# A hybrid decoder step on one core: norm of the first group on its products, banks and weight buffers shared out anew, two output projections moved forward

## The chip, the cores and the metric

The kernel runs on 1 core of a Trainium2 chip. The time is device microseconds of one execution; the kernel before has a median of 2943.49 us over 3 runs (2937.61 to 2943.66).

## What is computed

One layer of a decoder over 2048 prompt rows and 64 sample rows, in fp32. Sandwich norms stand around two sub-layers: a token mixer (windowed attention beside an RWKV-7 recurrence, both fed by one projection and joined by one output projection) and a gated FFN with a causal width-3 convolution. Cut to the lines that the change touches:

```python
hn = _rms_norm(x, g_pre_mix)
proj = hn @ w_in                       # q, k, v, and the RWKV columns
...                                    # attention, window 128; RWKV-7, state 64 x 64
mix = jnp.concatenate([o_attn, o_rw], axis=-1) @ w_out
x = x + _rms_norm(mix, g_post_mix)
f, new_conv = _conv_ffn(_rms_norm(x, g_pre_ffn), conv_prev, w_ffn_in, conv_w, conv_b, w_ffn_out)
x = x + _rms_norm(f, g_post_ffn)
```

`_rms_norm` divides each row by the root of its mean square and multiplies each column by a gain. The division is one factor per row, so it may as well be applied to the rows of `hn @ w_in`; the gain may not.

## The kernel before

**Tiling.** The 2112 rows are cut into five groups g0 to g4, four of 448 rows and one of 320. For each group there are stages: P (projection, 20 tiles), O (output projection, 8 tiles) and FFN, the latter as a main stage of 60 tiles and a last stage of 6. In the code `P[g]`, `O[g]`, `F[2g]` (main) and `F[2g+1]` (last); here P0 to P4, O0 to O4, F0 to F9. A tile is 24 matmuls: 8 steps of depth 128, each with three products (high and low halves of activations and weights, `split`, L348 to L351: ScalarE rounds, VectorE subtracts). `Dense.run` (L357) goes through the tiles in the order of the list `order` (L1581). It loads raw weights (`raw`, three buffers of tag "w"), splits them one tile ahead (`halves`, two buffers each of "wh" and "wl"), and splits the eight activation slices of the next stage while the last tile of the stage before runs (`piece`). Products are gathered in PSUM banks of tag "z" (two) in `gemm` (L433) and in `down` of the FFN, and the function `end` or `take` reads them out on ScalarE or VectorE.

**Mixer.** Eight units (256 prompt rows each, `Mixer.unit`) and one for the sample rows are written as generators. Their PSUM tiles have tag "a" (three banks) and "o" (two); tag "y" (one) serves the side work of the dense stages. That is 8 banks in all.

**Order of the work.** `Flow` decides while the program is written: after each step of a dense tile, `tick` (L254) may put in one step of side work and one of a mixer unit. A unit is paced over a window of the dense work (`windows`, L1588) and starts when the one before it is through. `force` (L266) runs side and mixer steps unpaced until a condition holds. Two tiles ahead of a stage `run` forces its conditions (L398 to L401): a P stage needs its norm's row factors (`"rb" in st`), an O stage needs the mixer units of its rows (L1579), an FFN stage needs its group's O stage done. The rest of an O or a last FFN stage (row norm, gain, residual, second norm; `rest`, L779 and L884) is side work: eight times about three VectorE instructions, then eight more. The instructions so written are then put in order per engine by a list scheduler with its own model of times, the earlier-written first among those that it takes to be ready; at run time each engine goes through its list strictly in order.

**Start.** `norm` of P0 (L472) loads x row-wise in pieces through three small buffers ("r"), squares and sums, takes the inverse roots, spreads them over partitions with a matmul (`rb_ps`), and only then are the first slices of the transposed x scaled by gain and row factor (`scale`, L503), split and multiplied.

**Names and lines.** L183 is every matmul, L350 and L351 the two halves of a split, L503 `scale`, L627 and L630 `shift` after a projection tile, L789 and L797 the rest of an O stage, L861 the FFN's `take`, L1219 the reading of attention scores out of PSUM, L956 the reading of the recurrence's.

Of the kernel before, what the change touches and what calls it, by code (L numbers as in the profile page):

```python
# [18 lines left out]
D = 1024  # L19
# [61 lines left out]
class Shared:  # L81
# [26 lines left out]
    def derived(self):  # L108
# [35 lines left out]
        self.nconv = cp.tile([128, NF, DB, 2], F32, name="nconv")  # L144
        self.zcar = cp.tile([128, NF, 2], F32, name="zcar")
# [154 lines left out]
class Stage:  # L300


    def __init__(self, n, cond=always, begin=None, cond2=always):
        self.n, self.cond, self.begin, self.cond2 = n, cond, begin, cond2
        self.fetch = self.piece = None
        self.tasks, self.xhi, self.xlo, self.raw = [], [], [], []

# [4 lines left out]
class Dense:  # L312
# [10 lines left out]
    def ps(self, name, tag="y"):  # L323
        return self.pp.tile([128, 512], F32, tag=tag, name=name, bufs={"z": 2, "y": 1}[tag])

# [6 lines left out]
    def W(self, name, shape=(D,)):  # L332
        return self.sp.tile([128] + list(shape), F32, tag="w", name=name, bufs=3)

# [22 lines left out]
    def run(self, stages):  # L357
# [18 lines left out]
        def halves(i):  # L376
            if i < nt and i not in parts:
                raw(i)
                parts[i] = [view(i, self.sp.tile([128, D], F32R, tag=x, name=x, bufs=2)) for x in ("wh", "wl")]
                self.split(*parts[i], raws[i])  # L380

        first = stages[0]
        first.begin()
        yield first.cond2
        for k in range(3):
            first.fetch(k)
        for j in range(3):
            raw(j)
        halves(0)
        for k in range(KT):  # L390
            first.piece(k)
            yield None
        for i, t in enumerate(tasks):
            n1, n2, n6 = [starts.get(i + j) for j in (1, 2, 6)]
            if n6 and n6.begin:
                n6.begin()
            if n2:
                yield n2.cond  # L398
                yield n2.cond2
                if n2.piece:  # L400
                    yield from self.hold()  # L401
                    for k in range(3):
                        n2.fetch(k)
            wh, wl = parts[i]
            for k, _ in enumerate(t.run(wh, wl)):
# [6 lines left out]
                yield None  # L412

    def source(self, s, src, then=None):


        def fetch(k):
            if k < KT:
                s.raw.append(self.r(s.n))
                self.nc.sync.dma_start(out=s.raw[k], in_=src(k))  # L420

        def piece(k):
# [3 lines left out]
            hi, lo = [self.sp.tile([128, GW], F32R, tag=z, name=z, bufs=9)[:, :s.n] for z in ("xhi", "xlo")]  # L426
            self.split(hi, lo, x)
            s.xhi.append(hi), s.xlo.append(lo)
            fetch(k + 3)

        s.fetch, s.piece = fetch, piece

    def gemm(self, s, src, end, m=None):  # L433


        def run(wh, wl):
# [3 lines left out]
            for k in range(KT):  # L440
# [3 lines left out]
                if k == KT - 1:  # L444
                    end(ps)
                yield

        s.tasks.append(Task(src, run, m))


    def project(self, g):
# [5 lines left out]
        if sample:  # L457
            segs.append(Seg(npr, NS, DB, DS, DS, npr // CH, sh.sshift, sh.nshift, sh.SEC))
        ks, st, left = [], {}, [0]

# [11 lines left out]
        def norm():  # L472
# [3 lines left out]
            cuts = [0, GW, 2 * GW, D]  # L476
            yield from self.hold()
            for i in range(nt):
                xts = []
                for x, y in zip(cuts, cuts[1:]):  # L480
                    xts.append(self.r(y - x))
                    nc.sync.dma_start(out=xts[-1][:w], in_=a["x"][t0 + w * i:t0 + w * i + w, x:y])
                yield 3000
                for j, xt in enumerate(xts):
                    nc.scalar.activation(out=xt[:w], in_=xt[:w], func=AF.Square, accum_out=ss[:w, j, i:i + 1])
            self.held = False
            yield 1000
            for j in range(2):
                v.tensor_tensor(out=ss[:w, 0, :nt], in0=ss[:w, 0, :nt], in1=ss[:w, j + 1, :nt], op=ALU.add)
            rsqrt(nc, self.sp, rs[:w, :nt], ss[:w, 0, :nt], 1.0 / D, RMS_EPS, nt, w, "nrp")  # L490
# [8 lines left out]

        S = Stage(n, begin=lambda: self.flow.spawn(norm()), cond2=lambda: "rb" in st)  # L500
# [4 lines left out]
        self.source(S, lambda k: a["xT"][:, k, t0:t0 + n], scale)  # L505

# [11 lines left out]
        def key(p):  # L518
            def end(ps):
                ks.append(self.shift(segs, p, ps, self.A("k", n)))  # L520
                if p == 3:
# [7 lines left out]
        def norms():  # L529
            k2s = []  # L530
            for p in range(4):
                k2s.append(self.B("k2", [n]))
# [69 lines left out]

        tile = lambda i, end: self.gemm(S, a["w_all"][i], end)
        self.gemm(S, a["w_l"][:, :, 0:64], lora, 64)
        for p in range(4):
            tile(p, key(p))
        self.gemm(S, a["w_l"][:, :, 64:160], gate, 96)
        tile(12, rotary(0))
# [199 lines left out]
    def ffn(self, g):  # L808
# [8 lines left out]
        def gate(f):  # L817
            def end(ps):
# [16 lines left out]
                if sample:  # L835
                    nc.gpsimd.tensor_copy(out=sh.nconv[:, f], in_=zs[:, :, DS:DS + 2])
                nc.scalar.activation(out=c, in_=c, func=AF.Silu)  # L837
# [74 lines left out]
    def finish(self):  # L912
        self.nc.sync.dma_start(out=self.a["o_conv"], in_=self.sh.zcar)
        self.nc.sync.dma_start(out=self.a["o_conv_s"], in_=self.sh.nconv)


class Mixer:
# [16 lines left out]
    def ps(self, name, tag="a"):  # L934
        return self.pp.tile([128, 512], F32, tag=tag, name=name, bufs={"a": 3, "o": 2}[tag])

# [624 lines left out]
def program(tc, nc, a, seq):  # L1561
    with tc.tile_pool(name="xd", bufs=1, space=DRAM) as xd, tc.tile_pool(name="dp", bufs=2, space=DRAM) as dp, \
# [6 lines left out]
        dn = Dense(sh, flow, (dnp, pd))  # L1569
        mx = Mixer(sh, dn, (mip, pm, dp))  # L1570
        with tc.high_priority(-100):
            sh.load(nc.sync, "sel", "blockones", "wkmask", "amask", "sink", "g_up", "smask", "samask", "ssink", "sshift", "gT", "cw", "sconv")
            sh.stacks(dn.W)
        gs, nu = groups(seq), seq // T
# [13 lines left out]
        windows = [(f(P[1], 0), f(P[1], 1)), (f(P[2], 0), f(P[2], 0.9)), (f(P[3], 0.3), f(F[0], 0.45)), (f(F[0], 0.45), f(F[0], 0.93)),  # L1588
                   (f(F[2], 0), f(F[2], 0.47)), (f(F[2], 0.47), f(F[2], 0.93)), (f(F[4], 0), f(F[4], 0.93)), (f(F[6], 0), f(F[6], 0.6))]
# [21 lines left out]
```

## Time and profile before

| | |
|---|---|
| median of 3 runs | 2943.49 us (2937.61 to 2943.66) |
| the profiled execution | 2943.48 us, its span 2941.7 us |
| TensorE matmul busy | 2775.8 us, 94% of the span, 16993 matmuls |
| VectorE busy | 1925.4 us, 65% |
| ScalarE busy | 1409.3 us, 48% |
| mean granted TensorE clock | 0.968 |

Busy time of TensorE is a union of pipelined instructions, so 94% is not 94% of its peak; what a stretch loses is better read from the number of matmuls in it. The granted clock is given as a share of 2.4 GHz; the other level is 1.2 GHz (0.5).

### The profile page before, as it was taken

How to read it: one execution, taken by the hardware profiler on the slowest of the kernel's cores; microseconds unless marked ns; L12 is line 12 of the kernel's file. 1: busy time of each engine (PE TensorE's matmuls, PEld its weight loads, DVE VectorE, ACT ScalarE, POOL GpSimd, SP SyncE). 2: the span in 40 equal slices, each digit the busy share in tenths (PEclk: the TensorE clock that was granted, in tenths of full speed). 3: DMA queues.
4: the chain of work that ended last, by engine and by line, in shares of the span. 5: the costliest groups of instructions: out<-in, count | busy, mean ns of one | idle time of the engine just before them, and what ended most of it. 6: DMA issues, size and time to landing. Idle time of an engine off the chain costs nothing.

```text
span 2941.7 us, 46311 instructions
## 1 busy us (share of the span) xinstructions
PE 2775.8 (94%) x16993; PEld 2358.6 (80%) x16993; DVE 1925.4 (65%) x3782; ACT 1409.3 (48%) x2644; POOL 250.9 (9%) x519
## 2 busy tenths in 40 slices
PE   6998998999999998989999997999998999998997
PEld 4877766777887897768879886889876888997997
DVE  5776885795584557966836568355586566458566
ACT  5455545546445344655553445443444443344443
POOL 1001010020000000210100000000000000101111
PEclk9998999999999999999999998999998999999998
DMA  6575645766444335655443445433346434346443
GB/s 197 167 213 155 185 135 163 219 197 184 148 136 131 119 125 178 195 157 166 126 134 116 136 147 164 147 112 117 123 126 212 136 110 125 108 137 215 151 146 116
DMA packets 311555, 446.59 MB, mean 152 GB/s; under 512 B 118664, under 2 KB 240424, under 8 KB 311312
## 3 DMA queue, kind: packets, MB, share of 16 engines
q1 hardware_dynamic: 310896, 443.48, 49.5%
q8 instruction: 134, 2.20, 0.3%
q14 instruction: 93, 0.76, 0.1%
q10 hardware_dynamic: 432, 0.16, 0.0%
HBM read 362.19 MB, written 76.97 MB: 149 GB/s over the span
## 4 chain that ended last, share of the span: by engine, by line
PE 76%; DVE 13%; DMA 4%; ACT 3%; issue 3%; SPq 1%; DVEq 0%; ACTq 0%; POOL 0%; POOLq 0%
PE gm L183 47%; PE pf L183 16%; PE pc L183 2%; DVE wl L351 2%; PE po L183 1%; DVE tmp L994 1%; DVE tt L995 1%; PE pz L183 1%; PE ppt L187 1%; DMA r<-od 1%; ACT wh L350 1%; PE sc_e L183 1%; PE pu L183 1%; PE pS L183 1%; PE ms L183 1%
## 5 line engine op out<-in xcount | busy, mean ns | idle before, releaser
L183 PE MATMUL gm<-xhi,wh 128*128 128x448 f32 (+3 forms) x2880 | 1063.8, 371 | 39.3 <-ACT xhi L350 20.1
L183 PE MATMUL gm<-xhi,wl 128*128 128x448 f32 (+3 forms) x2880 | 1039.6, 362 | 16.0 <-DVE wl L351 15.8
L183 PE MATMUL gm<-xlo,wh 128*128 128x448 f32 (+3 forms) x2880 | 1040.6, 362 | 4.3 <-DVE xlo L351 4.0
L350 ACT CAST wh<-w 128x1024 fp32r<-128x1024 f32 (+1 forms) x470 | 488.9, 1040 | 791.7 <-PE gm L183 386.0
L351 DVE TENSOR_TENSOR wl<-w,wh 128x1024 fp32r<-128x1024 f32 (+1 forms) x470 | 570.3, 1213 | 442.6 <-ACT wh L350 441.7
L183 PEld LDWEIGHTS gm<-xhi,wh 128*128 128x128 f32 (+2 forms) x2880 | 546.4, 190 | 121.8 <-ACT xhi L350 31.4
L183 PEld LDWEIGHTS gm<-xhi,wl 128*128 128x128 f32 (+2 forms) x2880 | 546.1, 190 | 74.7 <-DVE wl L351 23.8
L183 PEld LDWEIGHTS gm<-xlo,wh 128*128 128x128 f32 (+2 forms) x2880 | 546.8, 190 | 60.4 <-DVE xlo L351 13.0
L183 PE MATMUL pf<-hh,wh 128*128 128x448 f32 (+1 forms) x880 | 324.8, 369 | 20.7 <-DVE acc L861 20.1
L183 PE MATMUL pf<-hl,wh 128*128 128x448 f32 (+1 forms) x880 | 315.0, 358 | 0.0
L183 PE MATMUL pf<-hh,wl 128*128 128x448 f32 (+1 forms) x880 | 314.5, 357 | 0.0
L834 POOL COPY zcar<-zz 128x2 f32<-128x2 f32 x110 | 82.3, 749 | 1533.9 <-ACT zz L823 1533.9
L183 PEld LDWEIGHTS pf<-hh,wh 128*128 128x128 f32 x880 | 166.6, 189 | 47.1 <-DVE acc L861 24.7
L861 DVE TENSOR_TENSOR acc<-acc,pf 128x448 f32<-128x448 f32 (+1 forms) x200 | 117.8, 590 | 100.1 <-PE pf L183 98.9
L183 PEld LDWEIGHTS pf<-hh,wl 128*128 128x128 f32 x880 | 167.0, 190 | 13.2 <-issue 1.8
L183 PEld LDWEIGHTS pf<-hl,wh 128*128 128x128 f32 x880 | 167.0, 190 | 12.2 <-issue 2.2
L844 DVE TENSOR_TENSOR c<-c,gm 128x448 f32<-128x448 f32 (+1 forms) x110 | 65.2, 592 | 134.7 <-PE gm L183 109.2
L830 DVE SCALAR_TENSOR_TENSOR c<-zz,c_cw,c 128x448 f32<-128x448 f32 (+1 forms) x220 | 140.8, 640 | 16.3 <-ACT c L824 13.4
L837 ACT ACTIVATE c<-c 128x448 f32<-128x448 f32 (+1 forms) x110 | 61.2, 557 | 124.0 <-DVE c L830 91.7
L350 ACT CAST xhi<-r 128x448 fp32r<-128x448 f32 (+1 forms) x120 | 63.5, 544 | 91.3 <-DMA r<-xnd 33.4
L994 DVE TENSOR_TENSOR tmp<-gb,tt 64x31 f32<-64x31 f32 (+21 forms) x279 | 91.6, 328 | 12.0 <-DMA gb<-dgr 9.3
L995 DVE TENSOR_TENSOR tt<-tt,tmp 64x31 f32<-64x31 f32 (+21 forms) x279 | 92.0, 330 | 2.6
(261 smaller groups left out, 3098.7 us busy)
## 6 DMA issues: line engine op xcount, KB each, us to landing
w<-in_w SPq DMA_DIRECT2D x220, 512.0 KB
w<-in_w2q SPq DMA_DIRECT2D x100, 512.0 KB
w<-in_w_all SPq DMA_DIRECT2D x90, 512.0 KB
ab<-abd SPq DMA_DIRECT2D x66, 512.0 KB
w<-in_w_out SPq DMA_DIRECT2D x40, 512.0 KB
r<-in_xT SPq DMA_DIRECT2D x64, 224.0 KB
r<-od SPq DMA_DIRECT2D x32, 224.0 KB
x2d<-mx SPq DMA_DIRECT2D x32, 224.0 KB
```

Source lines behind the costliest of these rows:

```text
L183: return self.te.matmul(out, lhsT, rhs, **kw)
L187: return self.te.transpose(*args)
L350: self.nc.scalar.copy(out=hi, in_=src)
L351: self.nc.vector.tensor_tensor(out=lo, in0=src, in1=hi.bitcast(F32), op=ALU.subtract)
L830: v.scalar_tensor_tensor(out=c[:, :npr], in0=z[:, j:j + npr], scalar=cw(j), in1=c[:, :npr], op0=ALU.mult, op1=ALU.add)
L834: nc.gpsimd.tensor_copy(out=sh.zcar[:, f, :], in_=z[:, npr:npr + 2])
L837: nc.scalar.activation(out=c, in_=c, func=AF.Silu)
L844: v.tensor_tensor(out=c, in0=c, in1=ps, op=ALU.mult)
L861: v.tensor_tensor(out=accs[c], in0=accs[c], in1=ps, op=ALU.add)
L994: v.tensor_tensor(out=tm, in0=col, in1=row, op=ALU.mult)
L995: v.tensor_tensor(out=tt[:nb, w:, 0:w], in0=tt[:nb, w:, 0:w], in1=tm, op=ALU.subtract)
```

## The change

- Of the 8 PSUM banks, dense "z" gets three instead of two and the mixer's "a" two instead of three.
- Of the weight buffers, "wh" and "wl" get three each instead of two and are split two tiles ahead instead of one; raw "w" gets two instead of three and is loaded four tiles ahead in the list instead of three.
- P0's norm: the slices of transposed x are loaded at once into eight buffers of tag "A", scaled by the gain alone while they are split, and multiplied before the row factors are known. The row factors come from four whole-row loads into buffers that the mixer doesn't use yet, and each product of P0 is multiplied by them on its way out of PSUM (`normed`); a product that comes out before they are written is first copied to SBUF and scaled by side work. From the fourth tile on the last step of a tile forces them.
- The order of stages: O3 goes ahead of F4 and F5 (it stood between them), O4 ahead of F6 and F7.
- The windows of mixer units: unit 2 from 0.1 of P3 to 0.15 of F0, units 3 and 4 within F0, 5 and 6 within F2, 7 and the sample unit within F4. Before, units 2 and 3 ended in F0, 4 and 5 lay in F2, 6 in F4, 7 and the sample in F6.
- The sample's convolution state is written over its input instead of into a tile of its own, and temporaries at the start use a buffer of the mixer.

```diff
     def ps(self, name, tag="y"):
-        return ... bufs={"z": 2, "y": 1}[tag])
+        return ... bufs={"z": 3, "y": 1}[tag])
...
-        return self.sp.tile([128] + list(shape), F32, tag="w", name=name, bufs=3)
+        return self.sp.tile([128] + list(shape), F32, tag="w", name=name, bufs=2)
...
         first = stages[0]
+        for k in range(KT):
+            first.fetch(k)
+            if k in (2, KT - 1):
+                raw(k // 4)
         first.begin()
-        yield first.cond2
-        for k in range(3):
-            first.fetch(k)
-        for j in range(3):
-            raw(j)
         halves(0)
         for k in range(KT):
             first.piece(k)
-            yield None
+        yield None
+        halves(1)
+        for j in range(2, 4):
+            raw(j)
...
                 if k == 1:
-                    halves(i + 1)
-                    raw(i + 3)
+                    halves(i + 2)
+                    raw(i + 4)
...
+            if gain:
+                self.nc.scalar.activation(out=hi, in_=x, func=AF.Copy, scale=gain(k))
+                self.nc.vector.scalar_tensor_tensor(out=lo, in0=x, scalar=gain(k), in1=hi.bitcast(F32), op0=ALU.mult, op1=ALU.subtract)
...
+            def take(ps):
+                h = self.A("hs", n)[:ps.shape[0]]
+                def scaled(x):
+                    v.tensor_tensor(out=h, in0=x, in1=st["rb"][:ps.shape[0]], op=ALU.mult)
+                    end(h)
+                def wait():
+                    yield lambda: "rb" in st
+                    scaled(h)
+                if "rb" in st:
+                    scaled(ps)
+                else:
+                    nc.scalar.copy(out=h, in_=ps)
+                    side(wait())
...
+                xts = [self.spare(i)[:w] for i in range(nt)]
+                for i, xt in enumerate(xts):
+                    nc.sync.dma_start(out=xt, in_=a["x"][t0 + w * i:t0 + w * i + w, :])
...
     def ps(self, name, tag="a"):
-        return ... bufs={"a": 3, "o": 2}[tag])
+        return ... bufs={"a": 2, "o": 2}[tag])
...
-        order = [P[0], P[1], P[2], O[0], P[3], F[0], O[1], F[1], P[4], F[2], O[2], F[3], F[4], O[3], F[5], F[6], O[4], F[7], F[8], F[9]]
+        order = [P[0], P[1], P[2], O[0], P[3], F[0], O[1], F[1], P[4], F[2], O[2], F[3], O[3], F[4], F[5], O[4], F[6], F[7], F[8], F[9]]
...
-        windows = [..., (f(P[3], 0.3), f(F[0], 0.45)), (f(F[0], 0.45), f(F[0], 0.93)),
-                   (f(F[2], 0), f(F[2], 0.47)), (f(F[2], 0.47), f(F[2], 0.93)), (f(F[4], 0), f(F[4], 0.93)), (f(F[6], 0), f(F[6], 0.6))]
+        windows = [..., (f(P[3], 0.1), f(F[0], 0.15)), (f(F[0], 0.15), f(F[0], 0.53)),
+                   (f(F[0], 0.53), f(F[0], 0.93)), (f(F[2], 0), f(F[2], 0.47)), (f(F[2], 0.47), f(F[2], 0.93)), (f(F[4], 0), f(F[4], 0.5))]
...
-        flow.units.append((f(F[6], 0.55), f(F[6], 0.93), [mx.sample({("P", ng - 1)})]))
+        flow.units.append((f(F[4], 0.5), f(F[4], 0.93), [mx.sample({("P", ng - 1)})]))
```

## Rows read from the trace of the kernel before

**Rows 1.** The page: busy time by engine, and the granted clock in 40 slices.

```profile
PE 2775.8 (94%) x16993; PEld 2358.6 (80%) x16993; DVE 1925.4 (65%) x3782; ACT 1409.3 (48%) x2644; POOL 250.9 (9%) x519
PEclk9998999999999999999999998999998999999998
```

**Rows 2.** Stretches: start:end, length, busy us (count) by engine, clock, DMA share, GB/s.

```profile
0.00:48.30 48.30, 20.76 (x74) 14.30 (x75) 23.03 (x53) 25.36 (x59) 3.66 (x19) 0.96 0.67 203
140.90:322.00 181.10, 168.51 (x1122) 127.85 (x1121) 128.51 (x276) 98.40 (x223) 21.47 (x40) 0.92 0.64 179
322.00:511.70 189.70, 172.23 (x1171) 129.49 (x1169) 141.38 (x317) 95.95 (x201) 13.53 (x37) 0.96 0.56 160
511.70:716.90 205.20, 194.16 (x1025) 151.89 (x1026) 156.87 (x326) 110.71 (x229) 21.87 (x37) 0.94 0.64 195
716.90:1082.70 365.80, 365.09 (x2403) 313.46 (x2402) 216.71 (x399) 179.69 (x317) 27.38 (x47) 1.00 0.44 137
1145.30:1201.90 56.60, 45.53 (x223) 33.90 (x222) 49.62 (x130) 28.31 (x77) 0.89 (x4) 0.82 0.60 181
1728.20:1754.80 26.60, 26.60 (x132) 21.05 (x131) 23.68 (x54) 11.00 (x17) 0.03 (x1) 1.00 0.59 172
1754.80:1824.00 69.20, 47.82 (x198) 40.13 (x197) 65.12 (x164) 31.22 (x58) 1.11 (x5) 0.80 0.58 178
2202.50:2262.30 59.80, 50.96 (x362) 37.47 (x363) 39.68 (x87) 26.78 (x65) 0.56 (x1) 0.77 0.60 187
2656.10:2714.90 58.80, 45.47 (x261) 40.36 (x261) 52.74 (x116) 26.38 (x50) 13.59 (x17) 0.94 0.67 216
2000.00:2100.00 100.00, 100.00 (x490) 91.74 (x489) 49.13 (x61) 33.60 (x44) 7.72 (x12) 1.00 0.34 107
2750.00:2850.00 100.00, 99.93 (x680) 99.46 (x679) 62.33 (x106) 45.95 (x80) 16.56 (x42) 1.00 0.47 149
...
20.00:30.00 10.00, 5.44 (x12) 2.68 (x13) 7.38 (x15) 5.85 (x10) 0.00 (x0) 1.00 0.82 274
```

**Rows 3.** Timeline of 0 to 40 us: start, length, engine, what, idle before.

```profile
0.74 1.34 SPq L482 DMA_DIRECT2D r<-in_x  x3
3.70 0.58 ACT L485 ACTIVATE r<-r 112x448 f32<-112x448 f32 x1 [0.27 <-DMA r<-in_x]
...
22.32 1.86 PE L183 MATMUL rb_ps<-dg,c_ones 112*128 112x448 f32 x2 [22.32 <-DVE dg L492]
22.54 0.62 ACT L350 CAST wh<-w 128x512 fp32r<-128x512 f32 x1 [0.18 <-DMA w<-in_w_l]
...
26.42 1.01 PE L183 MATMUL gm<-xhi,wh 128*64 128x448 f32 x2 [2.24 <-ACT xhi L350]
...
29.84 0.37 PE L183 MATMUL gm<-xhi,wl 128*64 128x448 f32 x1
```

**Rows 4.** Timeline of VectorE where F3 ends and F4 begins.

```profile
1770.15 2.46 DVE L797 SCALAR_TENSOR_TENSOR mx<-mx,c_gT,rb 128x448 f32<-128x448 f32 x4
...
1779.92 0.61 DVE L861 TENSOR_TENSOR acc<-acc,pf 128x448 f32<-128x448 f32 x1
```

**Rows 5.** Waits of TensorE: who for whom, us in total, times, longest.

```profile
PE rb_ps L183 <- DVE dg L492: 24.2, 2, 22.3
...
PE pf L183 <- DVE acc L861: 20.1, 12, 9.2
PE gm L183 <- DVE wl L351: 15.8, 14, 4.1
PE gm L183 <- ACT h L627: 9.4, 9, 2.7
...
PE sc_e L183 <- DVE s L1219: 4.9, 1, 4.9
```

**Rows 6.** Timeline of TensorE at that last wait, in F1.

```profile
1172.74 2.07 PE L183 MATMUL sc_e<-ab 64*128 64x128 f32 x8 [4.89 <-DVE s L1219]
```

**Rows 7.** Groups by line: the reading of attention scores.

```profile
L1219 DVE SCALAR_TENSOR_TENSOR s<-sc,c_amask 128x512 f32<-128x512 f32 (+1 forms) x64 | 41.3, 663 | 9.8 <-PE sc L183 9.6
```

More of the change, by code (lines that the diff above doesn't have):

```diff
@@ L323, in ps @@
     def ps(self, name, tag="y"):
-        return self.pp.tile([128, 512], F32, tag=tag, name=name, bufs={"z": 2, "y": 1}[tag])
+        return self.pp.tile([128, 512], F32, tag=tag, name=name, bufs={"z": 3, "y": 1}[tag])
     def A(self, name, w, dt=F32):
@@ L411, in run, with source @@
                     self.held = k < KT - 1
-                yield None
-    def source(self, s, src, then=None):
+                yield c
+    def source(self, s, src, then=None, gain=None):
         def fetch(k):
             if k < KT:
-                s.raw.append(self.r(s.n))
+                s.raw.append(self.A("xt", s.n) if gain else self.r(s.n))
                 self.nc.sync.dma_start(out=s.raw[k], in_=src(k))
@@ L458, in project, with normed @@
             segs.append(Seg(npr, NS, DB, DS, DS, npr // CH, sh.sshift, sh.nshift, sh.SEC))
-        ks, st, left = [], {}, [0]
+        ks, st, left = [None] * 4, {}, [0]
+        late = g == 0
+        def normed(end):
+            def take(ps):
[8 more added lines that the diff above has]
+                    scaled(ps)
+                else:
+                    nc.scalar.copy(out=h, in_=ps)
+                    side(wait())
+            return take if late else end
         def side(gen):
@@ L476, in norm @@
             cuts = [0, GW, 2 * GW, D]
[L477 to L482, printed above, removed]
[L483 to L489 removed]
+            if late:
+                xts = [self.spare(i)[:w] for i in range(nt)]
+                for i, xt in enumerate(xts):
+                    nc.sync.dma_start(out=xt, in_=a["x"][t0 + w * i:t0 + w * i + w, :])
+                yield 3000
+                for i, xt in enumerate(xts):
+                    nc.scalar.activation(out=xt, in_=xt, func=AF.Square, accum_out=ss[:w, 0, i:i + 1])
+                yield 1000
+            else:
+                yield from self.hold()
+                for i in range(nt):
+                    xts = []
+                    for x, y in zip(cuts, cuts[1:]):
+                        xts.append(self.r(y - x))
+                        nc.sync.dma_start(out=xts[-1][:w], in_=a["x"][t0 + w * i:t0 + w * i + w, x:y])
+                    yield 3000
+                    for j, xt in enumerate(xts):
+                        nc.scalar.activation(out=xt[:w], in_=xt[:w], func=AF.Square, accum_out=ss[:w, j, i:i + 1])
+                self.held = False
+                yield 1000
+                for j in range(2):
+                    v.tensor_tensor(out=ss[:w, 0, :nt], in0=ss[:w, 0, :nt], in1=ss[:w, j + 1, :nt], op=ALU.add)
             rsqrt(nc, self.sp, rs[:w, :nt], ss[:w, 0, :nt], 1.0 / D, RMS_EPS, nt, w, "nrp")
@@ L498, in norm @@
             nc.scalar.copy(out=rb, in_=pb)
-        S = Stage(n, begin=lambda: self.flow.spawn(norm()), cond2=lambda: "rb" in st)
+        S = Stage(n, begin=lambda: self.flow.spawn(norm()), cond2=lambda: late or "rb" in st)
         def scale(k, x):
             v.scalar_tensor_tensor(out=x, in0=x, scalar=sh.vcol(V_GPRE, k), in1=st["rb"], op0=ALU.mult, op1=ALU.mult)
-        self.source(S, lambda k: a["xT"][:, k, t0:t0 + n], scale)
+        if late:
+            S.taken = 3, lambda: "rb" in st
+            self.source(S, lambda k: a["xT"][:, k, t0:t0 + n], gain=lambda k: sh.vcol(V_GPRE, k))
+        else:
+            self.source(S, lambda k: a["xT"][:, k, t0:t0 + n], scale)
         def lora(ps):
@@ L530, in norms @@
             k2s = []
+            yield lambda: None not in ks
             for p in range(4):
@@ L934, in ps @@
     def ps(self, name, tag="a"):
-        return self.pp.tile([128, 512], F32, tag=tag, name=name, bufs={"a": 3, "o": 2}[tag])
+        return self.pp.tile([128, 512], F32, tag=tag, name=name, bufs={"a": 2, "o": 2}[tag])
     def factors(self, c):
```

30 lines of the change are left out of this document (16 added, 14 removed).

## The prediction

> **What bounds the kernel now.** The page first: TensorE shows 94% busy, VectorE 65%, ScalarE 48%, and the granted clock dips in about ten of the 40 slices [rows 1]. TensorE is the bound, so the question is where it stands or runs at half its clock. Busy time does not tell that, since matmuls overlap; counts do. In a calm FFN stretch 490 matmuls of 448 columns take 100 us, 204 ns each, and in the last group 680 of 320 columns take 100 us, 147 ns each. The main stage F0 holds 60 tiles x 24 = 1440 such matmuls (294 us) and 963 others, mostly small ones of the mixer: (365.8 - 294) / 963 = 75 ns each [rows 2]. With these three prices every stretch has a time that it needs, and the rest is lost:
>
> - 0 to 48.3 us, three tiles: 72 x 0.204 = 14.7 us needed, **33.6 lost**.
> - P1, 181.1 us: 480 x 0.204 + 642 x 0.075 = 146.1, 35.0 lost. P2, 189.7: 97.9 + 691 x 0.075 = 149.7, 40.0 lost. O0 with P3, 205.2: 672 x 0.204 + 353 x 0.075 = 163.6, 41.6 lost. **117 in all.**
> - F3.4 to F4.4 (1754.8 to 1824), seven tiles: 34.3 + 30 x 0.075 = 36.6 of 69.2, 32.6 lost. F5.3 to F6.0, four tiles: 19.6 + 266 x 0.075 = 39.6 of 59.8, 20.2 lost. F7.4 to F8.7, two tiles of 448 columns and eight of 320: 9.8 + 28.2 + 1.6 = 39.6 of 58.8, 19.2 lost. **72 in all.** The four tiles ahead of the first of them, 96 + 36 matmuls, lose 26.6 - 22.3 = 4.3.
> - F1.4 to P4.1, four tiles (two of 320 columns): 26.4 of 56.6, 30.2 lost [rows 2].
>
> The timelines say why. At the start TensorE waits 22.3 us for the norm and has its first projection matmul at 26.4 us [rows 3]. At the three FFN boundaries an FFN stage follows directly on the last stage of another group, and its condition, an O stage done, is forced two tiles ahead. VectorE then gets eight L797 of the O stage's rest ahead of the FFN's own L861: the first four run from 1770.15, and an L861 comes at 1779.92 only; TensorE's banks are full meanwhile, for up to 9.2 us [rows 4, 5]. In P stages the named waits are shorter: for a bank that ScalarE has to read (h, 9.4 us in all) and for the second half of the weights (wl, 15.8) [rows 5].
>
> **The change part by part.** The sum starts from the profiled execution, 2943.48 us (span 2941.7 and some 1.8 around it), which is the median of the runs to 0.01.
>
> *Start: -20.* The first x pieces are issued at 0.74 and read at 3.70, so 2.3 us beside their 0.7 us of bytes, at 274 GB/s, the rate of 20 to 30 us [rows 2, 3]. Now the order is three slices of x (0.69 MB), the first weights (0.26), five slices (1.15), the next weights (0.52), then four rows-of-x loads (1.84). The first weights are there at 0.74 + 2.3 + 3.5 = 6.5 us, split by 7.8 (0.62 for wh [rows 3], about as much for wl), and the first tile starts near 8 instead of 26.4. The next weights land at 12.6, are split by 15, when the first tile, at half clock like the one now (0.37 us a matmul near 29.8 [rows 3]), is through. The third tile's weights wait for a buffer and are queued behind the rows of x: (4.46 + 0.52) MB at 274 is 18.2, so 21.2, split by 23.5. The fourth tile then starts at 28.4 instead of 48.3. If these weights went ahead of the rows it would be 24.9, a gain of 23. If the one in-order TensorE list has `rb_ps` ahead of the third tile, it waits for the rows (19.3), the last square, and the roots (5 us now): row factors near 27, gain 16. I take 20, ends 12 and 24. Of what the step adds, 20 multiplies of about 0.6 us on VectorE replace eight L503; that is 12 us over P0's 90, under VectorE's free third; uncovered it would be 7 us. The copy of the first product is one ScalarE instruction.
>
> The Trainium skill, "DMA: Bandwidth & Descriptors", section "Queues, rings and completion order", says that on each DMA engine descriptors are consumed in the order of the ring, and that SyncE owns one row of rings. By that rule the weights do come behind the rows of x and the gain is 20, without it 23; no row here shows two such loads overtaking each other or not.
>
> *Order of stages: -54.* F3, F5 and F7 are now followed by O3, O4 and F8, whose conditions are met before: O3 and O4 ask for mixer units, F8 for O4, which now lies a main stage back. F4 asks for O2, now with F3 and O3 between, and F6 for O3, with F4, F5 and O4 between. The eight L797 lose their forced place. What stays is VectorE's paced load, as in the four tiles ahead of the forced one, 4.3 us lost per boundary [rows 2], and the squares of O3 and O4 beside it; I take 6 each: 72 - 18 = 54. Ends: 40 (10 left at each and some of it shifted) and 67. O3's and O4's own slices of x still need the three small buffers that the rest holds; that wait ends with the rest's first half, near F3.4, so it costs little.
>
> *A third bank and earlier weights: -22.* A dense product may now wait one tile longer (4.9 us) for its reader, and wl is asked for a tile earlier. Outside the boundaries that addresses 9.4 + about 12 of wl [rows 5], and the half clock that follows: P1 to P3 have 0.92, 0.96 and 0.94 [rows 2], some 34 us of clock lost, of which the longest part, in P1, belongs to a forced mixer chain and stays. 21 + 20 addressed, half of it got; ends 8 and 40. The raw weights: their load now waits on SyncE for the wl of two tiles ahead, and loads and stores queued behind it wait too; but the wanted time is two tiles off (9.8 us), so I price it at nothing, and 5 us if a slow load eats that.
>
> *Two banks for the mixer: +20.* The trace has two-bank behaviour nowhere. Low end 0: with three, the only wait of size is 4.89 us in F1 [rows 6]. High end: I paired each of the 407 tiles of tag "a" with the last read of the tile two before it, in the order of the trace (for scores that reader is L1219, 64 times [rows 7]). 51 would have found the bank unread, by 77 us in sum, 38 of it in F1 to P4 and nearly none in FFN main stages. The scheduler, which knows of two banks, puts dense matmuls into such gaps; a quarter stays, 20, as in P stages where VectorE is 70 to 76% busy [rows 2] its model is least sure.
>
> *Denser units: +8.* Unit 2 gets most of its work into O0 and P3. P1 and P2 lose some 0.056 us per other matmul, FFN stages none [rows 2]; about 150 others moved there cost 8 (ends 0 and 15). Units 3 to 7 in main stages run at 75 to 85 ns wherever they lie: nothing. *Later pace: +4.* Before, the forced wait for the norm had moved the planner's clock some 9 us ahead, so that units came earlier; now unit 1 may end that much later ahead of O0 (ends 0 and 8). The tail, the last stage's rest, is untouched.
>
> Sum: -20 - 54 - 22 + 20 + 8 + 4 = -64, so 2943.5 - 64 = 2879.5, called **2880**.
>
> **The rivals.** *More (0.10):* all waits at the boundaries go and with them the half clock in P stages, and the scheduler hides the two banks: -23 - 67 - 40 + 5 + 8 = -117, about 2830. The boundaries' clock of 0.77 to 0.94 [rows 2] speaks for it, VectorE's load in P stages against. *The boundaries only move (0.14):* O3 and O4 come some 300 us earlier, and if units 6, 7 and the sample are not through, their serial chains are forced there. Each would then lose what F1.4 to P4.1 loses, 30 instead of 6: +48, about 2928. Against it: unit 6 has its window end in F2, six tiles ahead. *Two banks bind (0.10), slower:* on a saturated VectorE the scores of both streams wait for each other's reads, TensorE stands for all 77 us, and the clock falls with it: F1.4 to P4.1, with one long wait for a bank, lost 0.18 x 56.6 = 10 us to the clock [rows 2, 6]; some 28 over all four P stages, 105 instead of 20, so about 2965. It decides from 84 us on. F1's 4.89 us wait, already with three banks, at a clock of 0.82 [rows 2, 6] speaks for it; that the conflicts lie where few units are now planned, against. The Trainium skill, "Perfetto Trace Analysis", section "Optimization Strategy", says that a recurring gap on the engine that should be saturated can mean too little PSUM for the next tile; taken for the mixer it speaks for this rival, taken for dense products (L861 above) for the forecast. *The start gives nothing (0.04):* the row factors come so late that the fourth tile waits for them: 2900, within the range.
>
> **How the numbers follow.** Forecast 0.62 (its own range 2850 to 2910), the rivals as said. 2840 to 2930 takes in the moved boundaries and the ends of the unknown costs; outside lie the two-bank rival and most of "more", 0.18. About 0.2%, 6 us, is what can be told from no change: faster 0.62 + 0.10 + 0.12 + 0.02 = 0.86, same 0.04 from the edges of the last two, slower 0.10.
>
> **What would show it.** Start: first projection matmul near 8 us and the fourth tile near 28. Order: no row of L797 in a block ahead of L861; the tiles F3.4 to F3.5 near 5 us each and a clock of 1.0 there. Banks: waits for h and wl under 10 us together, and new waits of sc, sc_e, ppt or pz for L1219, L956 or pT, under 25 us. O3 and O4 must start without a run of pz and pc matmuls alone ahead of them. If those mixer waits exceed 80 us, or O3 stands, the forecast is wrong.

## The result, and the profile after

The changed kernel takes 2909.11 us (median of 4 runs, 2908.37 to 2913.12) beside 2940.55 us of the kernel before: a ratio of 0.9894, with an interval from 0.9881 to 0.9907. That is 31 us faster. It lies inside the range of 2840 to 2930, 29 us above the 2880 foretold. The profiled execution took 2909.42 us, its span 2907.6; the mean granted clock went from 0.968 to 0.973.

The page of the changed kernel: busy time by engine, and the granted clock in 40 slices, to lay beside [rows 1].

```profile
PE 2772.0 (95%) x16993; PEld 2354.7 (81%) x16993; DVE 1925.0 (66%) x3792; ACT 1409.1 (48%) x2628; POOL 239.3 (8%) x519
PEclk9997999989999999998999999999999999999998
```

The work is the same, only its place differs. So the comparison goes by stages. Here is the changed kernel by stretches: start:end, length, busy us (count) of TensorE, its weight loads, VectorE, ScalarE, GpSimd, then clock, DMA share and GB/s. The first four are P0, P1, P2 and O0 with P3 and F0; the next five F3, O3, F5, F7 and all of O2 to F7.

```profile
7.30:126.70 119.40, 113.90 (x507) 93.59 (x507) 88.19 (x149) 72.24 (x126) 12.18 (x36) 0.99 0.69 202
126.70:315.20 188.50, 169.60 (x1121) 128.30 (x1121) 127.47 (x266) 94.75 (x213) 11.79 (x38) 0.92 0.58 166
315.20:513.60 198.40, 181.33 (x1172) 133.24 (x1171) 144.64 (x324) 100.77 (x211) 18.45 (x39) 0.94 0.56 163
513.60:1149.20 635.60, 610.33 (x4060) 499.28 (x4060) 425.83 (x891) 331.63 (x652) 45.34 (x86) 0.98 0.51 154
1790.40:1835.10 44.70, 43.43 (x241) 34.10 (x239) 43.47 (x103) 22.40 (x46) 1.10 (x2) 1.00 0.62 191
1835.10:1890.60 55.50, 47.98 (x225) 40.44 (x224) 53.87 (x134) 26.98 (x57) 2.66 (x1) 0.91 0.64 204
2261.80:2291.20 29.40, 29.40 (x145) 26.93 (x144) 20.71 (x31) 11.61 (x17) 0.00 (x0) 1.00 0.48 149
2622.30:2651.50 29.20, 29.20 (x146) 26.95 (x145) 20.76 (x31) 11.68 (x17) 0.18 (x1) 1.00 0.48 154
1746.10:2651.50 905.40, 890.39 (x4951) 782.24 (x4950) 579.06 (x1041) 397.25 (x652) 56.08 (x101) 0.99 0.46 145
```

F3 fell from 57.2 us to 44.7, F5 from 68.9 to 29.4, F7 from 43.0 to 29.2, all three now at a clock of 1.00; F5 is shorter also because 268 mixer matmuls have left it. P1 and P2 rose from 370.8 to 386.9.

The waits of TensorE in the changed kernel (who for whom, us in total, times, longest), to lay beside [rows 5]:

```profile
PE gm L182 <- ACT wh L351: 18.9, 5, 7.5
PE gm L182 <- DVE wl L352: 14.6, 8, 7.4
PE gm L182 <- ACT h L674: 12.6, 4, 6.9
...
PE sc_o L182 <- DVE s L1266: 5.5, 1, 5.5
...
PE sc L182 <- DVE s L1266: 4.1, 6, 1.3
...
PE pf L182 <- DVE acc L908: 2.9, 4, 0.9
```

The wait of the FFN's products for L861 (now L908) is nearly gone: 20.1 us to 2.9. The waits for h and wl are not: 25.2 us before, 27.2 now, fewer but longer.

The table gives the length of the same stretches for every kernel below, from the first dense matmul of a stage to that of the next, in us; dense matmuls are those of the tiles (outputs gm and pf), and in brackets stand the others, mostly small ones of the mixer. The lengths are of one profiled execution each, which for "banks alone" is the fastest of ten and 5 us under its median, and for "weights put back" the slowest of ten and 8.5 us above. For "units alone" and the others in the old order, O2 to F7 is the same set of stages in its old sequence. "Units" are the windows of the mixer units.

| kernel | to P1 | P1, P2 | O0, P3, F0 | O1 to F2 | O2 to F7 | F8, F9 |
|---|---|---|---|---|---|---|
| before | 140.9 | 370.8 | 571.0 (1314) | 598.0 | 997.5 (1669) | 263.5 |
| order and units alone | 141.7 | 374.6 | 649.8 (1946) | 599.5 | 921.1 (1061) | 261.0 |
| units alone | 141.2 | 371.5 | 649.3 (1946) | 602.1 | 934.2 (1013) | 264.6 |
| start alone | 138.9 | 375.8 | 581.7 (1314) | 606.1 | 992.6 (1669) | 265.2 |
| banks alone | 140.2 | 369.2 | 570.9 (1314) | 605.0 | 996.1 (1677) | 260.2 |
| weights alone | 141.0 | 363.3 | 582.0 (1326) | 605.5 | 986.0 (1669) | 264.8 |
| **after** | 126.7 | 386.9 | 635.6 (1946) | 596.9 | 905.4 (1061) | 256.1 |
| order and units put back | 126.4 | 387.8 | 573.5 (1314) | 604.2 | 984.9 (1677) | 259.0 |
| start put back | 138.7 | 374.2 | 634.5 (1946) | 597.5 | 904.0 (1061) | 256.7 |
| banks put back | 133.0 | 371.0 | 645.5 (1958) | 596.7 | 918.6 (1061) | 259.0 |
| weights put back | 144.3 | 386.9 | 641.3 (1946) | 594.3 | 918.8 (1061) | 257.7 |

### The profile page after: what moved, and what is told of

Read it like the earlier page. It is cut to its first block, busy times and chain, and to the rows that moved or that the text cites. A ratio compares the mean times of both kernels' runs of the same rounds, so it can differ in the third digit from the quotient of the medians.

```text
span 2907.6 us, 46258 instructions
## 1 busy us (share of the span) xinstructions
PE 2772.0 (95%) x16993; PEld 2354.7 (81%) x16993; DVE 1925.0 (66%) x3792; ACT 1409.1 (48%) x2628; POOL 239.3 (8%) x519
## 4 chain that ended last, share of the span: by engine, by line
PE 75%; DVE 13%; DMA 5%; ACT 3%; issue 3%; SPq 1%; DVEq 0%; ACTq 0%
PE gm L182 46%; PE pf L182 16%; PE pc L182 3%; DVE wl L352 2%; PE po L182 2%; DVE tt L1042 1%; DVE tmp L1041 1%; PE pz L182 1%; PE ppt L186 1%; ACT wh L351 1%; PE sc L182 1%; PE pu L182 1%; DMA w<-in_w_all 1%; PE pS L182 1%; PE sc_e L182 1%
## 5 line engine op out<-in xcount | busy, mean ns | idle before, releaser
L182 PE MATMUL pf<-hh,wh 128*128 128x448 f32 (+1 forms) x880 | 317.8, 361 | 3.8 <-DVE acc L908 2.9
L881 POOL COPY zcar<-zz 128x2 f32<-128x2 f32 x110 | 74.4, 676 | 1547.6 <-ACT zz L870 1547.6
L908 DVE TENSOR_TENSOR acc<-acc,pf 128x448 f32<-128x448 f32 (+1 forms) x200 | 117.3, 589 | 103.4 <-PE pf L182 102.7
L1041 DVE TENSOR_TENSOR tmp<-gb,tt 64x31 f32<-64x31 f32 (+21 forms) x279 | 91.4, 328 | 3.6 <-DMA gb<-dgr 1.0
L1042 DVE TENSOR_TENSOR tt<-tt,tmp 64x31 f32<-64x31 f32 (+21 forms) x279 | 91.9, 329 | 2.8
```

Of the source, the lines that this page charges most:

```text
L182: return self.te.matmul(out, lhsT, rhs, **kw)
L881: nc.gpsimd.tensor_copy(out=sh.zcar[:, f, :], in_=z[:, npr:npr + 2])
L908: v.tensor_tensor(out=accs[c], in0=accs[c], in1=ps, op=ALU.add)
L1041: v.tensor_tensor(out=tm, in0=col, in1=row, op=ALU.mult)
L1042: v.tensor_tensor(out=tt[:nb, w:, 0:w], in0=tt[:nb, w:, 0:w], in1=tm, op=ALU.subtract)
```

## The experiments

All were timed in three rounds beside the kernel before; a ratio is to that, with its interval.

### The four parts, each alone on the kernel before

The order with its windows (`b_order`):

```diff
-        order = [... F[2], O[2], F[3], F[4], O[3], F[5], F[6], O[4], F[7], F[8], F[9]]
+        order = [... F[2], O[2], F[3], O[3], F[4], F[5], O[4], F[6], F[7], F[8], F[9]]
-        windows = [..., (f(P[3], 0.3), f(F[0], 0.45)), ..., (f(F[6], 0), f(F[6], 0.6))]
+        windows = [..., (f(P[3], 0.1), f(F[0], 0.15)), ..., (f(F[4], 0), f(F[4], 0.5))]
```

> The kernel before with the new order of stages and the new windows alone. Theory 1 (the order gave what the trace of the whole change shows, 46 to 51 us less lost from O2 on, and the denser units cost some 17 in O0 to F0): 25 to 45 us faster than before. Theory 2 (the cost in O0 to F0 comes from the two mixer banks and not from the denser units): 45 to 55 us faster.

The new start, with its buffers and the convolution state in place (`b_start`), the diff being that of the change:

```diff
+        for k in range(KT):
+            first.fetch(k)
+            if k in (2, KT - 1):
+                raw(k // 4)
         first.begin()
-        yield first.cond2
```

> The kernel before with the new start of P0 alone (norm on the products), and the convolution state in place. Theory 1 (the gain at the start is real, but part is given back within P0): 10 to 20 us faster. Rival (P0's later tiles eat it, or O0 waits for its mixer units whatever P0 does): within 5 us of before.

The banks (`b_banks`):

```diff
-        return ... bufs={"z": 2, "y": 1}[tag])
+        return ... bufs={"z": 3, "y": 1}[tag])
...
-        return ... bufs={"a": 3, "o": 2}[tag])
+        return ... bufs={"a": 2, "o": 2}[tag])
```

> The kernel before with three dense and two mixer banks alone. Theory 1 (the loss in the P stages comes from the weight buffers): 0 to 25 us faster. Theory 2 (it comes from the mixer's two banks): 5 to 30 us slower.

The weight buffers and their earlier split (`b_weights`):

```diff
-        ... tag="w", name=name, bufs=3)
+        ... tag="w", name=name, bufs=2)
-        ... tag=x, name=x, bufs=2)) for x in ("wh", "wl")]
+        ... tag=x, name=x, bufs=3)) for x in ("wh", "wl")]
-                    halves(i + 1)
-                    raw(i + 3)
+                    halves(i + 2)
+                    raw(i + 4)
```

> The kernel before with three buffers each of the split weights, two raw ones, and both asked for a tile earlier, alone. Theory 1 (ScalarE stands in its list for a raw load, and what reads PSUM stands behind it): 5 to 30 us slower, with some 40 to 80 us of ScalarE waiting for loads of w where before has none. Theory 2 (the weights only come earlier): 10 to 25 us faster.

**Measured.** Order and windows 1.0014 [1.0005, 1.0024], start 1.0046 [1.0028, 1.0063], banks 1.0024 [1.0015, 1.0034], weights 1.0016 [1.0005, 1.0027]. Each alone is slower, by 4, 14, 7 and 5 us (from the ratios, of 2942.8 us). They add up to +1.00%, 29 us, and together they give -1.06%, 31 us. So 60 us lie in how the parts act on each other, and no sum of parts costed alone could have found them. In the stretches, the order with its windows makes O2 to F7 76 us shorter and O0 to F0 79 us longer. Most of both is work that moved: 608 other matmuls left the one and 632 entered the other, at 85 ns each (worked out under "The windows alone") 52 and 54 us. So some 25 us are gained in O2 to F7, half of the 54 foretold of the order, and 25 are lost in O0 to F0. The start alone begins at 7.3 us and has P1 at 138.9, 2 us earlier than before.

### The four parts, each put back in the changed kernel

`a_order_back`, `a_start_back`, `a_banks_back` and `a_weights_back` take the changed kernel and undo one of the four diffs above.

> The changed kernel with the old order and the old windows: start, banks and weights together on the kernel before. If the parts add up as they did alone: 15 to 25 us slower than before, 2960. If banks and weights cover the start, as the runs without them suggest: 0 to 15 us faster than before, 2930 to 2943.

> The changed kernel with the old start of P0: order, windows, banks and weights on the kernel before. If the start is worth what P0 shows, 14 us: 2915 to 2930. If the parts add up as alone: 2895. If the gain comes from order, banks and weights together: 2905 to 2925, with O3 no longer than in the changed kernel (55 us).

> The changed kernel with two dense and three mixer banks, as before. Theory 1: 0 to 20 us slower than the changed kernel. Theory 2 (two mixer banks bind): 10 to 30 us faster.

> The changed kernel with the weight buffers and their lead as before (two of each half, three raw). Theory 1: 0 to 20 us faster than the changed kernel. Theory 2: 10 to 25 us slower.

**Measured.** Order and windows put back 0.9986 [0.9974, 0.9999], start 0.9874 [0.9855, 0.9893], banks 0.9954 [0.9936, 0.9971], weights 0.9993 [0.9981, 1.0004]. Against the 2909 us of the change that is +30, -1, +17 and +27 us by the medians (2939.36, 2908.09, 2926.5, 2936.49), or some 27, -6, 18 and 29 by the ratios; for the start the two intervals overlap. The start, for which 20 us were foretold, brings nothing that shows: with it put back the kernel reaches P1 12.0 us later (138.7 against 126.7) and O0 0.7 us earlier (512.9 against 513.6). The banks and the weights, foretold to cancel (+20 and -22), cost 17 to 29 us each when they are undone: the gain of the order stands on both.

*Weights.* The profile with the weights put back is 35.6 us longer than that of the change, more than the 27 of the medians. Of these, 17.6 us lie ahead of P1 (144.3 against 126.7): without the early split the new start loses what it gained, as it did alone. Here are the waits of TensorE with the weights put back, from 0 to 144.3 us; in the changed kernel wl stands at 1.0 us over P0.

```profile
PE gm L182 <- ACT wh L351: 10.2, 2, 7.5
PE gm L182 <- DVE wl L352: 6.6, 3, 5.6
PE gm L182 <- DVE k L675: 4.9, 1, 4.9
```

Another 19 lie where the units are dense and at the boundaries (5.7 and 13.4, the table); O3 alone takes 66.1 us instead of 55.5, and 70.6 with the order and units alone. P1 and P2 take the same 386.9 us.

*Banks.* With two dense banks, P1 starts 6.3 us later, O0 to F0 take 9.9 us more and O2 to F7 13.2; TensorE's waits for h, the readers of dense banks, are longer. The same kernel gains 15.9 us in P1 and P2, of which below. The waits of TensorE with the banks put back, in O0 to F0 (504 to 1149 us):

```profile
PE gm L182 <- ACT h L674: 15.7, 5, 8.1
```

In the changed kernel (513.6 to 1149.2 us) that row is:

```profile
PE gm L182 <- ACT h L674: 9.8, 2, 6.9
```

### The windows alone

`b_windows` gives the kernel before the new windows and leaves its order, to take the two halves of `b_order` apart.

```diff
-        windows = [..., (f(P[3], 0.3), f(F[0], 0.45)), ..., (f(F[6], 0), f(F[6], 0.6))]
+        windows = [..., (f(P[3], 0.1), f(F[0], 0.15)), ..., (f(F[4], 0), f(F[4], 0.5))]
```

> The kernel before, its own order of stages, with the new windows of mixer units alone: splits the order run. Theory 1 (denser units cost 25 to 30 us in O0 to F0, and the order gives about as much): 10 to 30 us slower than before, F0 some 25 to 35 us longer than the 0.085 us per other matmul moved into it explain. Theory 2 (the moved stages stand somewhere else, and density is free): within 8 us of before.

**Measured.** 1.0071 [1.0052, 1.0089]: 21 us slower, where the forecast had 8 for denser units. So the order itself is worth 4 - 21 = -17 us on the kernel before. In the changed kernel the two were not taken apart. The 632 matmuls that moved into O0 to F0 lengthen it by 78.3 us, 124 ns each, and take 63.3 us out of O2 to F7 (656 of them, 96 ns each). The main stages of the kernel before charge 75 to 96 ns for such a matmul, beside 1440 dense ones of 204 ns (293.8 us): F2 takes 390.0 us with 1134 others, so (390.0 - 293.8) / 1134 = 85, and in the same way F4 89 (344.6 us, 570), F6 96 (354.4, 631), F0 75; the mean is 86, and 85 is used here. So 78.3 - 632 x 0.085 = 24.6 us are lost beyond that price. In the changed kernel the same stretch has grown by 64.6 us, so 10.9 are lost. The third bank and the early weights pay there: put back, they cost 9.9 and 5.7 us in it. The price is uncertain: F4 and F6 begin within the boundaries that lose time [rows 2], and without those tiles (five and one) they come to 66 and 87 ns. At the 75 ns of the forecast, 30.9 and 17.2 us are lost.

### The raw weights, two buffers or three

In the changed kernel ScalarE waits for raw weights 75 us in all. Its waits for their loads, in the changed kernel:

```profile
ACT wh L351 <- DMA w<-in_w_all: 36.5, 20, 6.4
ACT wh L351 <- DMA w<-in_w: 31.5, 16, 4.9
ACT wh L351 <- DMA w<-in_w_out: 5.8, 3, 2.7
ACT wh L351 <- DMA w<-in_w2q: 1.2, 2, 0.8
```

Before, they came to 1.2 us. At one place TensorE seems to pay for it: in P3 (timelines of ScalarE and TensorE, start, length, what, idle before) the split waits 6.44 us for its load, the read of a dense bank (h, L674) stands behind it on ScalarE's list, with some 5 us of other work between (L768, L1236), and TensorE waits 6.91 us for that bank.

```profile
614.80 1.04 ACT L351 CAST wh<-w 128x1024 fp32r<-128x1024 f32 x1 [6.44 <-DMA w<-in_w_all]
...
621.99 0.74 PE L182 MATMUL gm<-xhi,wh 128*128 128x448 f32 x1 [6.91 <-ACT h L674]
```

A third raw buffer needs room, so `a_x8` first takes one of the nine buffers of activation halves, and `a_x8_raw3` then adds the raw buffer.

```diff
-        ... tag=z, name=z, bufs=9)[:, :s.n] for z in ("xhi", "xlo")]
+        ... tag=z, name=z, bufs=8)[:, :s.n] for z in ("xhi", "xlo")]
...
-        ... tag="w", name=name, bufs=2)
+        ... tag="w", name=name, bufs=3)
```

> The changed kernel with eight instead of nine buffers each of the split activation slices; the control for the next run, which needs the room. Both theories: within 8 us of the changed kernel, 2909.

> The same with three raw weight buffers instead of two, loads asked for four tiles ahead as in the changed kernel. Theory 1 (the raw buffers cost the P stages their time): 10 to 30 us faster than with two, and ScalarE's waits for loads of w fall from 74 us to under 20. Theory 2 (the two mixer banks do): within 5 us.

**Measured.** 0.9887 [0.9859, 0.9916] without and 0.9864 [0.9846, 0.9882] with the third buffer: 2907.45 and 2900.32 us, 7 us apart, with intervals that overlap. In the trace the waits fall to 19 us in all, of which these two rows are the most (third raw buffer):

```profile
ACT wh L351 <- DMA w<-in_w_all: 8.1, 6, 3.0
ACT wh L351 <- DMA w<-in_w: 6.8, 3, 3.8
```

So 56 us less of waits, on an engine that is busy for 48% of the span, were worth some 7 us, and by the intervals perhaps nothing; the forecast had priced them at 0 to 5. Nor was the load what TensorE paid for in P3: with the third buffer it still waits 4.45 us for h at that place, and P3 takes 176.1 us in both kernels.

### Units moved from O0 and P3 into F0

`a_win` asks where in O0 to F0 the units cost most. It is `a_x8_raw3` with unit 2 later and units 3 and 4 pushed together behind it: all three still end at 0.93 of F0. O0 and P3 lose mixer work to F0, and the sum stays.

```diff
-        windows = [..., (f(P[3], 0.1), f(F[0], 0.15)), (f(F[0], 0.15), f(F[0], 0.53)), (f(F[0], 0.53), f(F[0], 0.93)), ...
+        windows = [..., (f(P[3], 0.3), f(F[0], 0.35)), (f(F[0], 0.35), f(F[0], 0.65)), (f(F[0], 0.65), f(F[0], 0.93)), ...
```

> The changed kernel with three raw weight buffers (and eight of the activation slices, for room), unit 2 from 0.3 of P3 to 0.35 of F0, unit 3 to 0.65, unit 4 to 0.93: P3 and O0 hold less of unit 2, F0 as much in all. Theory 1 (units next to an O stage's rest in P3 cost most): 5 to 15 us faster than the same with the new windows, 2885 to 2895. Theory 2 (the cost lies in F0): same or slower.

**Measured.** 2889.32 us, 0.9813 [0.9792, 0.9833]: faster than both kernels, and than `a_x8_raw3`, whose interval it does not touch. The stretches O0 with P3, then F0, first of `a_x8_raw3`, then of `a_win`:

```profile
518.00:751.10 233.10, 215.72 (x1381) 169.18 (x1381) 177.93 (x383) 125.88 (x264) 20.01 (x39) 0.95 0.63 188
751.10:1149.90 398.80, 395.44 (x2680) 329.13 (x2679) 245.93 (x507) 206.11 (x387) 32.88 (x47) 1.00 0.45 136
516.20:727.60 211.40, 198.05 (x1112) 156.24 (x1111) 157.55 (x328) 113.34 (x232) 16.27 (x37) 0.94 0.65 193
727.60:1142.80 415.20, 413.46 (x2952) 342.63 (x2949) 267.63 (x562) 218.46 (x419) 25.91 (x49) 1.00 0.46 139
```

269 other matmuls have moved. O0 and P3 are 21.7 us shorter without them, 81 ns each, and F0 is 16.4 longer with them, 61 ns each. F0 holds more of them than in any other kernel here (1507), so it is not their number in a main stage that costs most. They cost more in O0 and P3, as the first theory of the expectation has it; that O0's rest in P3 is the reason was not tried by itself. Together O0 to F0 take 626.6 us, 5.3 less than in `a_x8_raw3` (631.9) and 9 less than in the changed kernel. The medians differ by 11 us; the rest of it is in stretches of a few us each, which one profile can't settle.

## Why the prediction came out as it did

The direction, the range and the bound (TensorE, standing at the FFN boundaries) were right. That the total came so near is in part luck: measured alone every part loses time, 29 us in sum, and the forecast, a sum of parts, had no term for the 60 us that lie between them. Taken by place, the terms came out so; the 24 matmuls that changed place on balance, 632 in and 608 out, make the last 2 us.

| term | foretold | found | read from |
|---|---|---|---|
| start | -20 | -14.2 | P1's start |
| later pace | +4 | +16.1 | P1, P2 |
| order of stages | -54 | -45.8 | O2 to F7, -92.1 + 608 x 0.085; F8, -5.4 |
| denser units | +8 | +10.9 | O0 to F0, 64.6 - 632 x 0.085 |
| banks and weights | -2 | -3.1 | O1 to F2, F9 |
| matmuls moved | 0 | +2.0 | 24 x 0.085 |
| sum | -64 | -34.1 | the spans |

Of the 30 us between the sums, 12 are by this table the later pace, 8 the order, 6 the start and 3 the units. But by place is not by cause: the row of the order holds what the windows did in O2 to F7, and every row holds what banks and weights did there. And the price of 85 ns divides two rows: at the forecast's 75 ns the order comes to -51.9 and the units to +17.2.

**Start.** The step itself was right: the first tile starts at 7.33 us (foretold near 8), and the fourth at 24.2, earlier than the 28.4 foretold: a gain of 24, the upper end. At P1 14.2 are left. The timeline of the changed kernel shows why (start, length, engine, what, idle before):

```profile
0.75 1.36 SPq L424 DMA_DIRECT2D xt<-in_xT  x3
...
2.15 0.68 SPq L375 DMA_DIRECT2D w<-in_w_l  x1
...
4.96 1.79 ACT L433 ACTIVATE xhi<-xt,c_vec 128x448 fp32r<-128x448 f32 x3
...
6.04 2.46 SPq L375 DMA_DIRECT2D w<-in_w_all  x2
6.66 0.62 ACT L351 CAST wh<-w 128x512 fp32r<-128x512 f32 x1
7.33 0.18 PEld L182 LDWEIGHTS gm<-xhi,wh 128*64 128x64 f32 x1 [7.33 <-ACT wh L351]
...
8.54 0.90 SPq L513 DMA_DIRECT2D xr<-in_x  x2
...
14.44 1.05 ACT L351 CAST wh<-w 128x1024 fp32r<-128x1024 f32 x1 [1.97 <-DMA w<-in_w_all]
```

The third tile's weights were not issued behind the rows of x. SyncE has both loads of w between 6.04 and 8.50, the rows from 8.54 on, and ScalarE splits the third tile's at 14.44 instead of after 21.2. So the forecast had the order of SyncE's list wrong, and its case of "weights ahead of the rows" (24.9) held. The rule of the Trainium skill ("DMA: Bandwidth & Descriptors", section "Queues, rings and completion order"), by which descriptors go in the order of the ring, is not tested by it: no load here had another ahead of it to overtake. One reading was wrong but cost little: the 0.37 us at 29.84 [rows 3] is the length of one matmul, and the next starts 0.21 later, so that is no half clock. The first tile of the changed kernel takes 7.0 us (7.33 to 14.32), its matmuls 0.37 apart until 11.6 and 0.20 apart after.

What failed is the sentence that the twenty multiplies lie under VectorE's free third. A multiply on VectorE now stands between each product and its reader on ScalarE, and ScalarE's list is in order:

```profile
51.02 2.94 DVE L588 RECIPROCAL d<-d 8x448 f32<-8x448 f32 x1
...
55.05 1.68 DVE L479 TENSOR_TENSOR hs<-gm,rb 96x448 f32<-96x448 f32 x3
...
55.77 0.67 ACT L668 ACTIVATE hm<-hs,omu 96x448 f32<-96x448 f32 x1 [7.45 <-DVE hs L479]
...
56.80 1.04 ACT L351 CAST wh<-w 128x1024 fp32r<-128x1024 f32 x1
...
57.89 0.48 PE L182 MATMUL gm<-xhi,wh 128*128 128x448 f32 x1 [2.10 <-ACT wh L351]
```

ScalarE waits 7.45 us for the multiply, the next weights stand behind that wait, and TensorE has none; the matmuls after it come every 0.37 us, at half clock. From the fourth tile to P1 it takes 102.5 us instead of 92.5, so that 10 of the 24 us are given back, more than the 7 set as the upper bound. TensorE's waits over 0.3 us in these tiles come to 4.5 us (none before), this one the longest; no run here takes the multiply out, so what the rest is made of stays open. With the free third of an engine, the bounds of 0 and 7 us bore on its busy time only, not on who queues behind it.

**Later pace.** This term had the wrong cause and a quarter of the size. The planner's clock was to delay unit 1 by the start's gain; two other things came. In P1 there is one stall. The chain of unit 0's inversion on VectorE (L1041, L1042) ends late, ScalarE waits 7.86 us for it with the next weights behind, and TensorE stands 7.46 us:

```profile
238.91 1.93 ACT L1045 COPY gb<-tt 64x1024 f32<-64x1024 f32 x1 [7.86 <-DVE tt L1042]
...
240.74 1.04 ACT L351 CAST wh<-w 128x1024 fp32r<-128x1024 f32 x1
...
241.83 0.74 PE L182 MATMUL gm<-xhi,wh 128*128 128x448 f32 x1 [7.46 <-ACT wh L351]
```

This stall of 7.5 to 8 us, here or as a wait of pz behind the same chain, is in all five profiles that have the new start, two mixer banks and early weights together (the change, order put back, and the three kernels of the raw buffers and windows). It is in none of those that lack one of the three. It and the half clock behind it make some 10 us (7.46, and 5.5 us at half speed up to 247.3, 2.7 lost). That is what the old start saves in P1: 174.0 us against 188.4, of which some 4 are 48 other matmuls that then fall into P2.

The stall is not the whole term. With three mixer banks P1 and P2 take 371.0 us, but P1 is only 1.7 shorter, P2 14.2. With the weights put back they take 386.9 as in the changed kernel, without the stall. In P2 the dense matmuls of the changed kernel are through at 492.0, and 21.6 us of unit 1's end follow with none until O0. TensorE waits 5.36 us of them for VectorE, which goes through the last norm of unit 1 (rsg) and P2's own side work in turn:

```profile
491.64 0.36 PE L182 MATMUL gm<-xhi,wl 128*128 128x448 f32 x1
...
497.36 1.83 PE L182 MATMUL pb<-b,c_blockones 128*128 128x448 f32 x2 [5.36 <-DVE rsg L53]
...
513.63 1.11 PE L182 MATMUL gm<-xhi,wh 128*128 128x448 f32 x2
```

Before, that run is 14.5 us; it is 13.5 with the weights put back, none with the banks put back, and the same 21.6 with the old start. So unit 1 does end bare ahead of O0, as the term said, and costs 7 us more than before; but it takes banks and weights together, and not the start. The two come to some 17 us, near the 16.1 found, though with the weights put back the same 16 us come otherwise, and how is open. Why the scheduler puts the stall only where all three meet was not tried; it would need its order changed by itself.

**Order.** Right in mechanism, by place 8 us short; taken apart from the windows it is worth 17 us on the kernel before, a third of what was foretold. The L797 block ahead of the FFN's readers is gone, F3 runs at full clock, and O3 and O4 start without a run of pz and pc alone. (Its tiles F3.4 and F3.5 take 11.3 and 6.6 us, not 5 each; with the 28 other matmuls that now lie between them, at 85 ns, they would need 12.2, and they lose 5.7.) But one block only moved. The forecast looked at the buffers that O3's slices need; F4's slices need them too, and F3's rest holds them, so that its second half is forced in O3. VectorE works through it, mixed with the inversion, before the second half of the next weights, which had been possible from 1865.15 on, where ScalarE is through with the first:

```profile
1865.12 0.67 DVE L939 SCALAR_TENSOR_TENSOR acc<-acc,c_gT,rb 128x448 f32<-128x448 f32 x1
...
1873.89 0.61 DVE L941 TENSOR_TENSOR acc<-acc,r 128x448 f32<-128x448 f32 x1
...
1876.11 1.21 DVE L352 TENSOR_TENSOR wl<-w,wh 128x1024 fp32r<-128x1024 f32 x1
...
1877.37 0.74 PE L182 MATMUL gm<-xhi,wl 128*128 128x448 f32 x1 [7.42 <-DVE wl L352]
```

A tile of 4.9 us took 16.6 here, and O3 as a whole 55.5 where its 192 dense and 30 other matmuls need 39.2 + 2.6: 13.7 lost, where 6 were allowed for a boundary. The term's own range, 40 to 67, held what the table shows for it.

**Denser units.** The price of 75 ns for every other matmul was the one of F0, the cheapest of the four main stages (75 to 96). And "units in main stages run at 75 to 85 ns wherever they lie: nothing" failed: alone the windows cost 21 us. The number moved into O0 and P3 was wrong too: 355 instead of about 150 (46 and 307 before, 94 and 614 now), at the forecast's own 0.056 us 20 us instead of 8. In the whole it is 10.9, inside the bounds of 0 to 15, because the other parts carry some of it; at 75 ns it would be 17.2, outside.

**Banks and weights.** The waits for the mixer banks that L1266 has to read came to 10.4 us (sc_o 5.5, sc 4.1, sc_e 0.8), where under 25 were foretold and the kernel before had 5.3 already; so the rival by which they bind fell. But that the two terms cancel failed in the whole. With the banks put back, P1 and P2 are 15.9 us shorter and the other stretches 32.1 longer (table). The first is near the 20 set for two mixer banks, but alone the banks do nothing there (369.2 us against 370.8), and what they bring is the run ahead of O0, not waits for a bank. What was foretold of h and wl, under 10 us together, failed: 27. The Trainium skill's reading of a recurring gap as too little PSUM ("Perfetto Trace Analysis", section "Optimization Strategy"), taken for dense products, fits the trace: with two dense banks the waits for h in O0 to F0 are 15.7 us, with three 9.8. It is five waits against two, one profile each.

**The rivals.** "The boundaries only move" came at one of three boundaries, at 7.42 us, and not by its own cause, a unit's forced chain: what stands there is the rest of F3. "The start gives nothing" had 0.04 and was right in its time for the part (the start put back changes nothing), by another way than the row factors: by the readers in P0 and the stall in P1. The fourth tile did not wait for them.

## What to carry to other kernels

Parts of a change that share a scheduler and in-order engines don't add: here four parts that each lose time alone (29 us in sum) gain 31 together, so undo each one in the whole before judging it. When an engine is inserted between a product and its reader, look at what queues behind that reader; the wait is paid there, not in the inserted engine's busy time. A gain ahead of a stretch can be lost in that stretch: here 12 us at P1 were gone at O0, so follow a gain to the end of the run before counting it.

## What the runs showed of the hardware

- A reciprocal of 8x448 on VectorE takes 2.94 us; a plain operation of the same shape in its chain (L590) 0.61. It holds every reader behind it.
- Small mixer matmuls among dense ones of 448 columns lengthen a main stage of the kernel before by 75 to 96 ns each, what they make wait included. 632 more in O0 to F0, with two dense banks, took 124 ns each; 269 moved in `a_win` saved 81 ns each in O0 and P3 and cost 61 in F0.
- In the stretch from 7.3 to 11.6 us the clock's column shows 1.00, but the matmuls there start every 0.37 us, as they do at the lower of the two levels, and every 0.20 us from 11.89 on. The trace's own record of the granted clock begins only at 11.77 us (before: at 29.74, where the same change of spacing lies), so the 1.00 ahead of it is no reading. At the start of a program go by the spacing. The stretch, and two matmuls in it, in the changed kernel:

```profile
7.30:11.60 4.30, 4.27 (x11) 2.40 (x12) 3.92 (x7) 3.24 (x6) 0.00 (x0) 1.00 1.02 385
...
9.00 0.58 PE L182 MATMUL gm<-xlo,wh 128*64 128x448 f32 x1
9.37 0.58 PE L182 MATMUL gm<-xhi,wl 128*64 128x448 f32 x1
```
